# Two pairs of experts through one-hot products, and the scattered rows read back ahead of the last expert's weights

## The chip, the cores and the metric

One core of one Trainium2 chip. The metric is the device time of one execution, in microseconds (us). Three runs of the kernel before gave 2037.6, 2043.89 and 2045.23 us, median 2043.89.

## What is computed

Two layers of a hybrid network work on 512 latent tokens and 256 context tokens of width 1024. Each layer has a mixer (neighbourhood attention, a gated linear recurrence, differential attention) and then a mixture of 32 experts. Layer 0 sends all 768 tokens through the experts, layer 1 (the last) only the 512 latent ones. Each token goes to two experts:

```python
    for l in range(DEPTH):
        last = l == DEPTH - 1
        ...
        if last:
            xl = xl + ga2 * hierarchical_moe(hl2.reshape(B * S, D), *moe_args).reshape(B, S, D)
        else:
            ...
            y = hierarchical_moe(jnp.concatenate([hl2.reshape(B * S, D), hc2.reshape(B * L, D)], axis=0), *moe_args)
            xl = xl + ga2 * y[:B * S].reshape(B, S, D)
            xc = xc + cga2 * y[B * S:].reshape(B, L, D)
    return rmsnorm(xl, g_final)
```

An expert is `w2 @ (silu(w1 x) * (w3 x))` with 512 hidden columns, so its weights are 6 MB, and both layers read all of them from DRAM.

## The kernel before

The residual `X` stays in SBUF as tiles of 128 tokens by 1024 columns, six in layer 0 and four in layer 1. The experts run in an order `seq`, worked out from how many rows each may get (its capacity, 128, 64 or 32). This text counts experts by their place in that order: 0 to 31. The last ones have capacity 32, and two neighbours of these, such as 28 and 29 or 30 and 31, share a `Group` of 64 rows.

**The loop over experts** (L1973 to L2080) issues in pass n the weights of expert n (`load`, L1812 to L1823, through `eparts`, L1015 to L1026) and computes expert n-1. SP issues all these transfers from one queue: six parts of 1 MB per expert (two of w1, two of w3, two of w2), each into the next tile of a rotation `wcycle` (L1008), 16 tiles in layer 0 and 18 in layer 1. A part waits until the tile 16 or 18 places back has been used. The last expert's w2 is cut by halves of the output columns instead of halves of the rows. In layer 1 the load of expert 31 also fetches the vector `g_final`, whose tile comes from the same memory (L1820 to L1823).

**An expert** is a first product on TensorE (`first`, matmuls of w1 and w3 into `pss`), a copy to SBUF on ScalarE (`mid`), a transposition through TensorE with the activation and the product of the two halves (`hidden`; DVE writes `hT`, L1678), and a second product with w2 (`second`). `out` weighs the rows by the routing weight, into `u`.

**The rows get back to their tokens in two ways.** A `Group` with a `slot` sends its rows `u` with an indirect DMA from POOL to a DRAM buffer `yd` with two places per token (`send`, L1515 to L1518). A `Group` without one splits its rows into a high and a low part (`split`: cast on ScalarE L434, subtraction on DVE L435), makes a one-hot matrix of 64 rows by all tokens (`hots`, L1584), and multiplies the two (`product`, L1590): one product of 128 tokens by 512 columns per half tile into PSUM (`acc`, `po`), which DVE adds into `X`. For an inner group that is `add` (L1593 to L1602), a generator put on `queue`, which `fill` runs a step at a time between the matmuls of the expert after; for the last pair it is `combine` (L2094 to L2099) at the very end. Before the change only the last pair (30, 31) goes this way.

**The read-back** (L1986 to L1991) brings `yd` back after all scatters: six transfers of 1 MB in layer 0, four in layer 1, each with the two places of a tile's tokens. DVE adds them to `X` at L2110 to L2112, two adds of 128 by 1024 per tile, 12 and 8 in all.

**What sets the order.** Each engine runs its own instructions in a fixed order. Around the end of layer 0 it is spelled by a string (`LTS`, L63): a letter is a step of the last two experts, and `c` is `fill(1)`. In layer 1 the general code (L2054 to L2080) spreads the steps. The end of the last expert is `end` (L1745 to L1755): per column half a ScalarE copy L1752, a DVE add L1753, the weighing and the split, and then the 12 or 8 products of `combine`. In layer 0 two chunks of the next layer's input weights (`chunk`, L390) are loaded behind the read-back; ScalarE casts them and POOL subtracts (L435), on the engine that also makes the next layer's norm factors `rsx` (L406 to L409), from which DVE makes `dg` (L571) and ScalarE `hf` (L600) for the next layer's input product (L491).

Of the kernel before, what the change touches and what calls it, by code (L numbers as in the profile page):

```python
# [23 lines left out]
NE = 32  # L24
# [85 lines left out]
LAM = (1, 1)  # L110
DIAG = (1, 1)
SCT = (1, 1)
YLB = (3, 3)
WPRE = (4, 3)
WPS = ("ss", "sa")
# [135 lines left out]
def program(tc, a, out, dbg=None):  # L251
# [24 lines left out]
    Y = nc.sync  # L276
# [11 lines left out]
    yd = [dr.tile([2 * n_, D], F32, name=f"yd{l}") for l, n_ in enumerate((NT, NL))]  # L288
# [55 lines left out]
    def wtile(pool=None, n=6, dt=F32):  # L344
        return (pool or wt).tile([128, 2048], dt, name="w", bufs=n)
# [85 lines left out]
    ct = lambda c_, x_, y_: x_ if c_ else y_  # L431
# [20 lines left out]
    for l in range(2):  # L452
        last = l == 1
# [553 lines left out]
        wcount, held = [0], [None]  # L1007
        wcycle = [(lambda: wta, NWA[l])] * NWA[l] + [(lambda: wt2, nw2)] * nw2 + [(lambda: wt3, 4)] * 4  # L1008
# [478 lines left out]
        slots = wk_.tile([128, ncol], I32, name="slots") if SCT[l] else None  # L1487
# [21 lines left out]
        def place(s):  # L1509
            return s if s < nm else nm + (s - nm) // 2 if s < nr else s - np_  # L1510

        def column(s):
            return idn[:, place(s), :]
# [458 lines left out]
        gfin, es, early, backs = [], [], [], {}  # L1972
        for n_ in range(NE + 1):  # L1973
            f = None
            if n_ < NE:
                s = seq[n_]
                load(n_)
                if small_[0] is not None:
                    g, small_[0] = small_[0], None
                else:  # L1980
                    g = Group(column(s), slots[:, place(s):place(s) + 1] if SCT[l] and n_ < NE - 2 else None)
                    small_[0] = g if capacity(l, s) == 32 else None
                f = make(n_, g)
                es.append(f)
                g.apart = APT[l] and n_ >= NE - 2
            if n_ == NE - 1 and SCT[l]:  # L1986
                for t in ct(last, (0, 1, 2, 3), (4, 5, 0, 1, 2, 3)):
                    pl, nb = wcycle[wcount[0] % len(wcycle)]
                    backs[t] = wtile(pl() if callable(pl) else pl, nb).rearrange("p (c f) -> p c f", c=2)
                    wcount[0] += 1  # L1990
                    Y.dma_start(backs[t], yd[l].rearrange("(c t p) d -> t p c d", c=2, p=128)[t])  # L1991
            if n_ == NE - 1:
                mark.clear()
                if not last:
# [22 lines left out]
            nb = {32: 2, 64: 4, 128: 8}[e.cap]  # L2017
# [145 lines left out]
```

## Time and profile before

| what | value |
|---|---|
| runs | 2043.89, 2045.23, 2037.6 us; median 2043.89 |
| profiled execution | 2047.19 us, span 2045.6 us |
| PE (TensorE matmul) | 1692.9 us busy, 83% |
| DVE (VectorE) | 901.0 us, 44% |
| ACT (ScalarE) | 575.3 us, 28% |
| POOL (GpSimd) | 407.1 us, 20% |
| expert weights | 382 transfers of 1 MB |
| read-back | 10 transfers of 1 MB |
| scatters | 47 indirect DMAs, 44.3 us on POOL |

Spans and starts are microseconds from the start of the profiled execution's span. An engine's busy share is over the whole span. A row of a timeline has a start and a duration; what stands in brackets behind it is how long the engine had been idle and what ended that.

### The profile page before, as it was taken

To read this page: it belongs to the slowest core of one execution; us is meant where nothing else is said; L and a number is where in the kernel's file an instruction comes from. 1 tells how busy PE (TensorE), PEld (TensorE's weight loads), DVE (VectorE), ACT (ScalarE), POOL (GpSimd) and SP (SyncE) were. 2 spreads that over 40 slices of the span, in tenths; PEclk is the share of its full clock that TensorE was granted. 3 is DMA by queue.
4 is the path that set the end of the run, shared out by engine and by line. 5 is a ranking of instruction groups with operands and counts; after the bars stand their busy time and mean duration, and the time that the engine had idled before them with its cause. 6 is when DMAs were issued, how large, how long until landed. Compare 5 with 4: busy or idle time off the path is not lost. (4 is left out here: it accounts for less than half of the span.)

```text
span 2045.6 us, 24880 instructions
## 1 busy us (share of the span) xinstructions
PE 1692.9 (83%) x9306; PEld 975.2 (48%) x9306; DVE 901.0 (44%) x1506; ACT 575.3 (28%) x1033; POOL 407.1 (20%) x394
## 2 busy tenths in 40 slices
PE   4998998899697888889895987887959988879773
PEld 3766666676333333333333977566733333333221
DVE  3876443785622212212227698548662122121225
ACT  3563343662111101111113475346411010010011
POOL 1344000443311011001003145104321110010001
PEclk8999999898698998999896989898969989999886
DMA  8537967606799989989986113346469999999994
GB/s 299 203 131 285 322 225 185 165 37 252 275 409 348 407 344 368 417 325 410 401 342 261 58 51 103 125 111 207 188 228 400 404 414 409 410 413 416 416 392 167
DMA packets 153709, 579.20 MB, mean 283 GB/s; under 512 B 18734, under 2 KB 54958, under 8 KB 114672
## 3 DMA queue, kind: packets, MB, share of 16 engines
q1 hardware_dynamic: 142240, 553.35, 71.5%
q0 software_dynamic: 9328, 20.87, 2.9%
q10 hardware_dynamic: 2016, 3.34, 0.5%
q8 instruction: 75, 1.23, 0.2%
q14 instruction: 50, 0.41, 0.1%
HBM read 544.74 MB, written 42.05 MB: 287 GB/s over the span
## 5 line engine op out<-in xcount | busy, mean ns | idle before, releaser
L491 PE MATMUL mm<-hh,w 128*128 128x256 f32 (+1 forms) x960 | 191.5, 343 | 6.6 <-ACT w L434 4.7
L1643 PE MATMUL pss<-w,xT 128*64 128x512 f32 x368 | 170.7, 611 | 7.3 <-DMA w<-in_w_dram 7.3
L1642 PE MATMUL pss<-w,xT 128*64 128x512 f32 x368 | 175.3, 619 | 0.0
L1638 PE MATMUL pss<-w,xT 128*32 128x512 f32 x880 | 140.4, 686 | 37.2 <-DMA w<-in_w_dram 37.2
L491 PEld LDWEIGHTS mm<-hh,w 128*128 128x128 f32 x960 | 150.1, 193 | 37.7 <-issue 9.8
L1826 POOL DMA_INDIRECT xg<-h2d,idx_t x64 | 61.4, 959 | 515.7 <-PE mm L1628 476.8
L1648 PE MATMUL pss<-w,xT 128*128 128x512 f32 x352 | 156.0, 597 | 0.0
L1658 ACT COPY hs<-pss 128x512 f32<-128x512 f32 x53 | 30.9, 582 | 375.6 <-PE pss L1638 221.9
L1517 POOL DMA_INDIRECT yd<-yl,slots x47 | 44.3, 942 | 383.1 <-DVE yl L1562 204.3
L1700 PE MATMUL pss<-w,hT 128*64 128x512 f32 x184 | 102.0, 698 | 9.2 <-DVE hT L1678 8.9
L1648 PEld LDWEIGHTS pss<-w,xT 128*128 128x128 f32 x352 | 65.3, 190 | 89.1 <-issue 83.3
L1678 DVE TENSOR_TENSOR hT<-hT,mm 128x128 f32<-128x128 f32 (+1 forms) x53 | 18.3, 345 | 196.0 <-ACT hT L1677 195.9
L1701 PE MATMUL pss<-w,hT 128*64 128x512 f32 x184 | 102.0, 698 | 0.0
L1558 DVE SCALAR_TENSOR_TENSOR yl<-g,wsl,yl 64x1024 f32<-64x1024 f32 (+2 forms) x32 | 40.8, 1276 | 129.9 <-ACT yl L1553 129.6
L1638 PEld LDWEIGHTS pss<-w,xT 128*32 128x32 f32 x880 | 32.0, 122 | 137.7 <-issue 74.5
L1553 ACT ACTIVATE yl<-g,wsl 64x1024 f32<-64x1024 f32 (+2 forms) x32 | 36.6, 1147 | 211.2 <-DMA yd<-yl,slots 178.6
L1706 PE MATMUL pss<-w,hT 128*128 128x512 f32 x176 | 91.0, 664 | 3.1 <-issue 3.1
L491 PE MATMUL mm<-hl,w 128*128 128x256 f32 (+1 forms) x480 | 93.2, 336 | 0.1
L1562 DVE TENSOR_TENSOR yl<-pss,yl 64x512 f32<-64x512 f32 (+1 forms) x44 | 29.6, 687 | 138.7 <-PE pss L1701 76.0
L351 DVE COPY xT<-mm 128x512 f32<-128x512 f32 (+1 forms) x64 | 36.2, 566 | 101.2 <-PE mm L1628 100.5
L491 PEld LDWEIGHTS mm<-hl,w 128*128 128x128 f32 x480 | 75.4, 190 | 11.1 <-issue 0.8
L1643 PEld LDWEIGHTS pss<-w,xT 128*64 128x64 f32 x368 | 48.8, 140 | 60.3 <-issue 48.2
(377 smaller groups left out, 3263.4 us busy)
## 6 DMA issues: line engine op xcount, KB each, us to landing
w<-in_w_dram SPq DMA_DIRECT2D x382, 1024.0 KB
w<-in_w_ada_dram SPq DMA_DIRECT2D x48, 1024.0 KB
w<-in_w_in_dram SPq DMA_DIRECT2D x20, 1024.0 KB
yd<-bm SPq DMA_DIRECT2D x20, 512.0 KB
w<-yd SPq DMA_DIRECT2D x10, 1024.0 KB
ks<-st SPq DMA_DIRECT2D x16, 384.0 KB
w<-in_w_out_dram SPq DMA_DIRECT2D x5, 1024.0 KB
h2d<-hp SPq DMA_DIRECT2D x10, 512.0 KB
```

The lines of the kernel that those rows point to most:

```text
L491: i_ = T.matmul(o, x_(k), y_(k), start=(n == 0), stop=(n == 23))
L1517: G.indirect_dma_start(out=yd[l][0:2 * nrow, :], out_offset=bass.IndirectOffsetOnAxis(ap=idxt, axis=0), in_=rows, in_offset=None, bounds_c ...
L1553: S.activation(self.u[r], g2[r, 1], AF.Copy, scale=b_)
L1558: (V if eng[1] == "V" else G).scalar_tensor_tensor(self.u[r], g2[r, 0], a_, self.u[r], op0=ALU.mult, op1=ALU.add)
L1638: T.matmul(ph[32 * g:32 * g + 32, 0:512], xT[:, k + g // 2, 0:32], w(k + g // 2), start=(k == 0), stop=(k == 6))
L1642: T.matmul(ph[0:64, 0:512], xT[:, k, 0:64], w1(k), start=(k == 0), stop=(k == 7))
L1643: T.matmul(ph[64:128, 0:512], xT[:, k, 0:64], w3(k), start=(k == 0), stop=(k == 7))
L1648: T.matmul(ph[:, o:o + 512], xT[:, k, :], w(k), start=(k == 0), stop=(k == 7))
L1700: T.matmul(py[0:64, :], hT[:, k, 0:64], w2(k, 0), start=(k == 0), stop=(k == 3))
L1701: T.matmul(py[64:128, :], hT[:, k, 0:64], w2(k, 1), start=(k == 0), stop=(k == 3))
L1706: T.matmul(self.p[:, 512 * hf:512 * hf + 512], hT[:, k, :], w2(k, hf), start=(k == 0), stop=(k == 3))
L1826: G.indirect_dma_start(out=o[0:n_, :], out_offset=None, in_=h2d[l][0:nrow, :], in_offset=bass.IndirectOffsetOnAxis(ap=idxt, axis=0), bound ...
```

## The change

A constant `LATE` of 4 for both layers replaces the 2 that decides which experts get no `slot`: the pair (28, 29) now also goes through one-hot products, by the inner way (`add` on `queue`). Its rows are no longer sent to `yd`. The loop that issues the read-back moves from behind `load` of the last expert to ahead of it, in the same pass, and takes its tiles of the rotation there. Lines of the changed kernel behind the new constant are one higher.

```diff
@@ -110,6 +110,7 @@
+LATE = (4, 4)
@@ -1972,23 +1973,23 @@
         for n_ in range(NE + 1):
             f = None
+            if n_ == NE - 1 and SCT[l]:
+                for t in ct(last, (0, 1, 2, 3), (4, 5, 0, 1, 2, 3)):
+                    pl, nb = wcycle[wcount[0] % len(wcycle)]
+                    backs[t] = wtile(pl() if callable(pl) else pl, nb).rearrange("p (c f) -> p c f", c=2)
+                    wcount[0] += 1
+                    Y.dma_start(backs[t], yd[l].rearrange("(c t p) d -> t p c d", c=2, p=128)[t])
             if n_ < NE:
                 s = seq[n_]
                 load(n_)
                 if small_[0] is not None:
                     g, small_[0] = small_[0], None
                 else:
-                    g = Group(column(s), slots[:, place(s):place(s) + 1] if SCT[l] and n_ < NE - 2 else None)
+                    g = Group(column(s), slots[:, place(s):place(s) + 1] if SCT[l] and n_ < NE - LATE[l] else None)
                     small_[0] = g if capacity(l, s) == 32 else None
                 f = make(n_, g)
                 es.append(f)
                 g.apart = APT[l] and n_ >= NE - 2
-            if n_ == NE - 1 and SCT[l]:
-                for t in ct(last, (0, 1, 2, 3), (4, 5, 0, 1, 2, 3)):
-                    pl, nb = wcycle[wcount[0] % len(wcycle)]
-                    backs[t] = wtile(pl() if callable(pl) else pl, nb).rearrange("p (c f) -> p c f", c=2)
-                    wcount[0] += 1
-                    Y.dma_start(backs[t], yd[l].rearrange("(c t p) d -> t p c d", c=2, p=128)[t])
             if n_ == NE - 1:
```

Three places where the order of instructions moves. First DVE at the end of layer 0's experts, before: `hT` of L1678 is the last expert's hidden activation, L1753 its two output halves, L2112 the adds of the read-back, L2099 those of the last pair's products.

```order
L1584 TENSOR_SCALAR w<-cs_83,idn 128x128 x2
L1678 TENSOR_TENSOR hT<-hT,mm 128x4x32
L1753 TENSOR_TENSOR yl<-pss,hs 32x512
L1562 TENSOR_TENSOR yl<-yl 32x512
L1753 TENSOR_TENSOR yl<-pss,hs 32x512
L435 TENSOR_TENSOR w<-yl,w 32x512
L2112 TENSOR_TENSOR X<-X,w 128x1024
L1562 TENSOR_TENSOR yl<-yl 32x512
L2112 TENSOR_TENSOR X<-X,w 128x1024 x2
L2099 TENSOR_TENSOR X<-X,pss 128x512
```

The same place of the changed kernel (L1602 is the add of an inner group's product, L2113 that of the read-back):

```order
L2113 TENSOR_TENSOR X<-X,w 128x1024
L1679 TENSOR_TENSOR hT<-hT,mm 128x4x32
L1602 TENSOR_TENSOR X<-X,acc 128x512
L1602 TENSOR_TENSOR X<-X,po 128x512
L2113 TENSOR_TENSOR X<-X,w 128x1024 x9
L1754 TENSOR_TENSOR yl<-pss,hs 32x512
L1563 TENSOR_TENSOR yl<-yl 32x512
L1754 TENSOR_TENSOR yl<-pss,hs 32x512
L1563 TENSOR_TENSOR yl<-yl 32x512
L436 TENSOR_TENSOR w<-yl,w 32x512 x2
L2100 TENSOR_TENSOR X<-X,pss 128x512 x2
```

Nine adds of the read-back now stand between the last expert's `hT` and its output halves; before, all twelve stood behind the second half.

PE at the same place. Before, the last expert's first product (`pss<-w,xT` x16) is followed at once by its hidden step (`mm<-cst,hs`):

```order
L267 MATMUL pss<-w,hT 32x512 x8
L267 MATMUL pss<-w,xT 32x512 x16
L267 MATMUL mm<-cst,hs 128x64 x8
L267 MATMUL pss<-w,hT 32x512 x8
L267 MATMUL pss<-w 128x512 x2
```

In the changed kernel:

```order
L268 MATMUL acc<-yl,oneh 128x512
L268 MATMUL po<-yl,oneh 128x512
L268 MATMUL pss<-w,xT 32x512 x16
L268 MATMUL acc<-yl,oneh 128x512
L268 MATMUL po<-yl,oneh 128x512
...
L268 MATMUL mm<-cst,hs 128x64 x8
L268 MATMUL acc<-yl,oneh 128x512
L268 MATMUL po<-yl,oneh 128x512
L268 MATMUL pss<-w,hT 32x512 x8
```

Of the pair's twelve products two stand ahead of the last expert's first product, eight (three pairs are left out) between it and the hidden step, two behind that.

SP at the end of layer 1's experts. Before:

```order
L1024 DMA w<-in_w_dram 128x2x1024
L1822 DMA w<-in_g_final_dram 128x1024
L1818 TENSOR_LOAD sid
L1024 ISA
L1024 DMA w<-in_w_dram 128x2048
...
L1024 DMA w<-in_w_dram 128x4x512
L1991 DMA w<-yd_65 128x2x1024 x4
```

In the changed kernel:

```order
L1025 DMA w<-in_w_dram 128x2x1024
L1981 DMA w<-yd_65 128x2x1024 x4
L1823 DMA w<-in_g_final_dram 128x1024
L1819 TENSOR_LOAD sid
L1025 ISA
L1025 DMA w<-in_w_dram 128x2048
```

The four read-backs stand ahead of `g_final` and of the last expert's six parts. In layer 0 the six read-backs move likewise.

## Rows read from the trace of the kernel before

**Rows 1.** The page: DMA in 40 slices of the span.

```profile
DMA  8537967606799989989986113346469999999994
```

**Rows 2.** Windows at layer 0's end: PE, PEld, DVE, ACT, POOL, clock, DMA share, GB/s.

```profile
1060.00:1076.00 16.00, 13.96 (x127) 6.54 (x126) 8.00 (x17) 3.95 (x8) 0.91 (x1) 1.00 1.02 408
1076.00:1096.00 20.00, 10.50 (x34) 3.18 (x33) 10.73 (x16) 2.67 (x5) 0.00 (x0) 0.62 1.03 405
1096.00:1106.00 10.00, 2.42 (x4) 0.98 (x4) 10.00 (x11) 1.87 (x3) 1.30 (x14) 0.50 0.08 27
```

**Rows 3.** Windows at the end of layer 1's experts.

```profile
1985.00:2008.00 23.00, 15.09 (x96) 6.04 (x91) 4.65 (x8) 3.54 (x7) 0.00 (x0) 0.85 1.01 407
1997.00:2002.00 5.00, 4.48 (x24) 1.18 (x27) 0.00 (x0) 0.00 (x0) 0.00 (x0) 0.50 1.03 405
2008.00:2015.00 7.00, 3.34 (x17) 0.86 (x11) 3.46 (x5) 1.77 (x3) 0.00 (x0) 1.00 0.31 128
```

**Rows 4.** DMA issues from 1900 to the end: transfers, KB each.

```profile
w<-in_w_dram SPq DMA_DIRECT2D x33, 1024.0 KB
```

**Rows 5.** Waits of SP's queue, 1044 to 1110: total, times, longest.

```profile
SPq L1991 <- DMA yd<-yl,slots: 14.1, 1, 14.1
```

**Rows 6.** Timeline of POOL, 1044 to 1070: start, duration, line.

```profile
1047.65 0.92 POOL L1517 DMA_INDIRECT yd<-yl,slots  x1 [5.02 <-DVE yl L1562]
1067.54 0.91 POOL L1517 DMA_INDIRECT yd<-yl,slots  x1 [18.98 <-DVE yl L1562]
```

**Rows 7.** Timeline of PE, layer 0: expert 31's first product, hidden, second product.

```profile
1070.65 3.62 PE L267 MATMUL pss<-w,xT 128*32 128x512 f32 x32
1075.50 2.04 PE L267 MATMUL mm<-cst,hs 128*128 128x64 f32 x16 [1.23 <-ACT hs L1658]
1078.22 3.63 PE L267 MATMUL pss<-w,hT 128*32 128x512 f32 x8 [0.69 <-DVE hT L1678]
```

**Rows 8.** Timeline of DVE, layer 0: last expert's output and the adds into X.

```profile
1082.56 0.68 DVE L1753 TENSOR_TENSOR yl<-pss,hs 32x512 f32<-32x512 f32 x1 [4.39 <-ACT hs L1752]
1090.99 2.36 DVE L2112 TENSOR_TENSOR X<-X,w 128x1024 f32<-128x1024 f32 x2
1102.83 0.68 DVE L2099 TENSOR_TENSOR X<-X,mm 128x512 f32<-128x512 f32 x1
1114.76 0.69 DVE L2099 TENSOR_TENSOR X<-X,po 128x512 f32<-128x512 f32 x1 [1.70 <-PE po L267]
```

**Rows 9.** Groups by line on DVE, 1060 to 1118: the one-hot matrix.

```profile
L1584 DVE TENSOR_SCALAR w<-cs,idn 128x128 fp32r<-128x128 f32 x6 | 1.3, 274 | 0.0
```

**Rows 10.** By source line: the read-back adds, and products (min/median/max ns).

```profile
L2112 DVE TENSOR_TENSOR X<-X,w x20: 1215/1219/1226, 1089.0 to 2025.9; 128x1024 f32<-128x1024 f32 x20
L1590 PE MATMUL acc<-yl,oneh x2: 393/593/793, 2014.8 to 2026.1; 128*128 128x512 f32 x2
```

**Rows 11.** Groups by line on POOL, 1080 to 1118: busy, mean ns, idle before.

```profile
L435 POOL TENSOR_TENSOR w<-w 128x2048 fp32r<-128x2048 f32 x2 | 9.1, 4540 | 0.9 <-ACT w L434 0.9
```

**Rows 12.** Timeline of ACT and PE: first hf, then layer 1's steady input product.

```profile
1114.40 0.56 ACT L600 ACTIVATE hf<-mm,scol,acol 128x256 f32<-128x256 f32 x1
1127.40 0.36 PE L491 MATMUL mm<-hh,w 128*128 128x256 f32 x1
```

**Rows 13.** Window of layer 1's input product, just behind.

```profile
1128.00:1143.00 15.00, 15.00 (x128) 15.00 (x128) 6.97 (x30) 6.68 (x14) 1.83 (x3) 1.00 0.01 1
```

**Rows 14.** Timeline of PE, layer 1: experts 30 and 31.

```profile
1980.68 5.43 PE L1638 MATMUL pss<-w,xT 128*32 128x512 f32 x30 [2.13 <-DMA w<-in_w_dram]
1997.52 6.00 PE L1638 MATMUL pss<-w,xT 128*32 128x512 f32 x30 [3.91 <-DMA w<-in_w_dram]
```

**Rows 15.** Timeline of DVE, layer 1: second output half, first finished tile.

```profile
2012.90 0.69 DVE L1753 TENSOR_TENSOR yl<-pss,hs 32x512 f32<-32x512 f32 x1 [1.85 <-ACT hs L1752]
2027.07 0.68 DVE L2099 TENSOR_TENSOR X<-X,mm 128x512 f32<-128x512 f32 x1
```

**Rows 16.** Timeline of SP's queue, layer 1: parts 2 to 6 of expert 31.

```profile
1983.24 3.55 SPq L1024 DMA_DIRECT2D w<-in_w_dram  x5
```

## The prediction

> **What bounds the kernel now.** I read the span in 40 slices first. The DMA is full through the experts of layer 1 (9s from slice 31 to 39) and through the end of layer 0's (8s and 9s up to slice 21) [rows 1], so at both places where the change acts the weights come as fast as the queue carries them. The windows say when that ends. In layer 0 the share is 1.03 until 1096 and 0.08 in the 10 us after: the transfers end near 1096.8 [rows 2]. In layer 1 it is 1.01 until 2008 and 0.31 after, so the last bytes land near 2014 [rows 3]. The timelines give the rest: in both layers the last expert's first product waits for its weights, and behind it stands a tail in which DVE never rests long: in 1096 to 1106 it is busy 10.00 of 10.00 us [rows 2]. So two things count: when the last expert's weights are there, and how much DVE work stands behind them on the path.
>
> **The change part by part.** The sum is made against the profiled execution, 2047.19 us with a span of 2045.6, which stands 3.3 us above the median of the runs. T1 is the end of the last expert's first product: 1070.65 + 3.62 = 1074.27 in layer 0 [rows 7], 1997.52 + 6.00 = 2003.52 in layer 1 [rows 14].
>
> *(a) Layer 0, weights later.* Six read-backs, 6.29 MB, now go ahead of expert 31's six parts. At 405 to 408 GB/s [rows 2] that is 15.4 us; the pair's 64 rows of 4 KB are not written to DRAM any more, 0.26 MB or 0.6 us. T1: +14.8, to 1089.1. The wait of 14.1 us in which SP held the read-back for the pair's scatter [rows 5] gives nothing back: the queue was full meanwhile [rows 2], because 31's parts stood ahead of it. Now the read-back waits for expert 27's scatter instead, issued at 1047.65. The pair's was issued at 1067.54 [rows 6] and let the read-back go some 6 us later by the end of that wait, so I take 1054 for 27's; the queue's backlog then is several parts of 2.6 us each (1.05 MB at 405 GB/s), so it should not run dry.
>
> *(b) Layer 0, T1 to the first output half.* Before, L1753 ends at 1082.56 + 0.68 = 1083.24 [rows 8], 9.0 us after T1. Now PE has eight one-hot products before the hidden step. They alternate between two PSUM tiles, so DVE's adds pace them, which start 0.6 us apart where they run back to back (0.68 busy [rows 8], ends overlapping): 5.4 us with the first product. Then hidden 2.04 [rows 7], ACT and DVE 0.6 together, one more pair of products and adds 1.8, then the nine read-back adds that stand ahead of L1754 on DVE, 2.36 for two [rows 8] or 1.18 each: 10.6, and L1754 itself 0.68. Sum 21.1, so +12.1.
>
> *(c) Layer 0, first output half to the first complete residual tile.* Before, 1083.24 to 1102.83 + 0.68 = 1103.51 [rows 8], 20.3 us, with nine of the twelve read-back adds mixed in, 10.6 us. Without them, and with about 1 us of it lost again, 10.7 remain: the second half, the splits, the first products' adds and waits for ScalarE. So -9.6, and the tile is complete at 1120.8, +17.3.
>
> *(d) Start of layer 1.* Before, the last add ends at 1115.45 [rows 8], the first `hf` runs at 1114.40, and the steady input product only from 1127.40 [rows 12]. Between lie two chunk splits on POOL, 9.1 us [rows 11], ahead of which the norm factors could not pass. The chunks land near 1097 as before (the queue carries the same bytes), but now DVE and ScalarE get to the last tiles later than that, so the splits are over when the norm factors are wanted. I take -9.4 of it as recovered. Ends: nothing recovered (0), and all of POOL's 9.1 with the last add's own shift of only 11.4 (its read-back adds are gone), which nets +2.3 for layer 0. The value taken lies near the second end, because both splits lie on the path before. What is left is not absorbed later: PE is busy 15.00 of 15.00 us right behind [rows 13]. **Layer 0: 14.8 + 12.1 - 9.6 - 9.4 = +7.9**, bounds +2.3 and +17.3.
>
> *(e) Layer 1, weights later.* 33 parts and the read-backs share one queue here [rows 4]. Four read-backs go ahead: 4.19 MB at 407 GB/s [rows 3] is 10.3, less 0.6 for the scatter: +9.7, T1 = 2013.2.
>
> *(f) Layer 1, T1 to the first finished tile.* Before, the second half's L1753 ends at 2013.59, 10.1 after T1, and the first tile is done at 2027.75, 24.2 after T1 [rows 15]. Between the two DVE also does eight read-back adds, 1.18 each, 9.4 us. In the changed order all eight stand ahead of the last expert's `hT`, while PE still waits for weights. 10.1 + 5.3 = 15.4: -8.8. The final norm and the stores are as before. **Layer 1: +0.9**; bounds -2.5 (the first adds of the tail also come earlier) and +2 (half of a part's 2.6 us lost, see the queue below).
>
> *Covered, at nothing.* The six one-hot matrices, 1.3 us on DVE [rows 9], the pair's splits, the first two products, and three of layer 0's twelve read-back adds run while PE waits for 31's weights; without that cover they would cost 1.3, some 3, 1.2 and 3.6 us. In layer 1 the pair's eight products, 0.6 us each [rows 10], stand on PE behind the first matmul of expert 30's first product, paced by adds: about 5 us. That product waits for weights before (2.13 us, start 1980.68) and should end some 5 us later, near 1991 instead of 1986 [rows 14]. Its cover is the queue: 31's product starts at 1997.52 and would come 10 us later.
>
> **Queues passed.** The read-backs pass 31's parts on SP, and in layer 1 `g_final`'s load. That load takes a tile that expert 30's first product must have released. Before, part 2 of expert 31 was held until 1983.24 for such a tile [rows 16]; now `g_final` is held until near 1989, and all six parts stand behind it. Engines still have the backlog of 30's parts and four read-backs, several us beyond that: I take no loss.
>
> **The clock.** In layer 0, 31's product takes 3.62 us in a window of granted clock 1.00, the full 2.4 GHz [rows 2, 7]; in layer 1 a like one takes 6.00 at 0.50, 1.2 GHz, behind a PE that had waited for weights [rows 3, 14]. After the change PE waits in layer 0 too. I add nothing, since only the product's last quarter stands behind the last part, 0.6 us at most. The Trainium skill, page "TensorE: Matmul & The Clock Gate", Part 1, calls the lower clock the default, which sustained activity releases. By it the extra one-hot products on PE would argue for the full clock, and the sum would be about 1 us less; the rows here agree as far as they show the low level after waiting.
>
> **Sum.** +7.9 + 0.9 = +8.8: the profiled execution would be 2056.0, and the median 2043.9 + 8.8 = **2052.7 us**.
>
> **Rivals.**
>
> *No net change.* The start of layer 1 recovers everything it can (+2.3) and layer 1's end gains 2.5: about 2043.9. For it: 9.1 us of POOL on the path [rows 11], and transfers end when they ended before. Against it: (a) and (b) are added in a fixed order, and DVE is the engine of the tail. If the moved adds do nothing at all, it is the same number.
>
> *Slower by much: `g_final` blocks SP.* In layer 1 its load waits for expert 30's first product, which stands behind eight paced products; if that ends beyond about 1998, when the queue's backlog is eaten, every us after it delays all of expert 31 fully. Some 9 us of it, and the forecast, give 2062 or more. For it: SP was held at this tile before [rows 16]. Against: backlog of about four read-backs. The same price holds in layer 0, if 27's scatter lands past 1060.
>
> *Faster: the adds leave both tails for nothing.* If the last expert's weights were not late on the path, 20 adds of 1.18 us, 23.6, would go from the tails [rows 10]: 2043.9 - 23.6 = 2020.3. For it: DVE is full in layer 0's tail [rows 2]. Against: the queue is full, so six MB ahead must cost 15 us, and the order puts nine adds back. The Trainium skill, page "DMA: Bandwidth & Descriptors", Rules for kernel authors, says to issue a transfer early, compute, and wait late. By that rule the early read-back is right and this rival holds; the rows speak against it, with a share of 1.03 that leaves no free transfer time [rows 2].
>
> **How the numbers follow.** Forecast (net +0 to +16): 0.62. No net change: 0.20. Blocked queue: 0.12. Faster: 0.06. The range 2040 to 2062 leaves out the faster rival, the blocked queue and a little of the forecast's own upper end. Its low end is the no-change case less 3.9, its high end the forecast with nothing recovered (+9.4). A measurement tells about 0.5%, 10.2 us, from no change: faster is below 2033.7, slower above 2054.1. The forecast's 0.62 splits into 0.36 within and 0.26 above, since 2052.7 lies just inside. Same: 0.36 + 0.20 = 0.56. Slower: 0.26 + 0.12 = 0.38. Faster: 0.06.
>
> **What would show it.** In the changed kernel's profile: 31's first product ending near 1089 and 2013; nine back-to-back read-back adds in layer 0 right ahead of L1754, near 1099 to 1110; L1602 adds paced at 0.6 us ahead of the hidden step; chunk splits on POOL before the last adds, and the steady input product near 1135; `g_final`'s issue near 1989 and the DMA share still about 1.0 up to 2008. The prediction is wrong if T1 of layer 0 comes before 1084, if the nine adds run before 31's first product ends, if the input product starts by 1128, or if the DMA runs dry between 1985 and 2010.

## Result and profile after

The changed kernel took 2065.4 us (median of four runs, 2060.07 to 2074.64) against 2044.45 before; the ratio is 1.0101, 95% interval 1.0066 to 1.0136. It is slower by about 1%: 21 us between the medians, 13.5 to 27.8 us by the interval, where 8.8 were forecast. The profiled execution took 2064.35 us (span 2062.7) against 2047.19: 17.2 us more.

Executions of one kernel differ by several us before they even reach the place of the change (103 runs of the kernel before, made with the experiments below, lie between 2032.82 and 2064.15), so the traces are compared from marks close by. In layer 0 these are the start of the last gather of an expert's rows on POOL (1041.70 before, 1040.56 after), T1, the end of the first output half, the end of the first row of adds from `mm` ("tile"), and the start of the first eight steady matmuls `mm<-hl,w` of layer 1 ("steady"). In layer 1 they are its last gather (1945.43 and 1960.99), T1, tile and the end of the span. All in us:

| kernel | gather to T1 | to output half | to tile | to steady | **layer 0** | gather to T1 | to tile | to end | **layer 1** |
|---|---|---|---|---|---|---|---|---|---|
| before | 32.6 | 9.0 | 20.3 | 24.1 | 85.9 | 58.1 | 24.2 | 17.9 | 100.2 |
| forecast shift | +14.8 | +12.1 | -9.6 | -9.4 | +7.9 | +9.7 | -8.8 | 0 | +0.9 |
| changed | 47.9 | 29.6 | 12.6 | 13.6 | 103.6 | 68.7 | 16.1 | 16.9 | 101.7 |
| measured shift | +15.3 | +20.6 | -7.7 | -10.5 | +17.7 | +10.6 | -8.1 | -1.0 | +1.5 |

Layer 1 came out within 1 us of what was worked out, and in layer 0 three of four steps did within 2 us. The second step is 8.5 us larger than forecast, and layer 0 as a whole 9.8 us, so it is nearly the whole error there. The windows of the changed kernel there answer [rows 2]:

```profile
1076.00:1096.00 20.00, 13.41 (x61) 5.98 (x57) 15.22 (x25) 2.30 (x4) 0.00 (x0) 0.84 0.98 382
1096.00:1106.00 10.00, 4.63 (x13) 1.38 (x12) 9.06 (x6) 4.44 (x4) 7.15 (x2) 0.67 0.00 2
1106.00:1116.00 10.00, 0.00 (x0) 0.00 (x0) 10.00 (x6) 0.00 (x0) 3.79 (x13) 0.50 0.31 105
```

From 1106 to 1116 DVE is busy all the time and every other compute engine waits for it, with POOL busy beside it until 1109.4. DVE's timeline, columns as in [rows 8] (L2113 are the read-back adds, L1679 writes the last expert's `hT`, L1754 its first output half):

```profile
1093.94 1.22 DVE L2113 TENSOR_TENSOR X<-X,w 128x1024 f32<-128x1024 f32 x1
1096.93 0.29 DVE L1679 TENSOR_TENSOR hT<-hT,mm 128x128 f32<-128x128 f32 x1 [1.78 <-ACT hT L1678]
1098.36 18.91 DVE L2113 TENSOR_TENSOR X<-X,w 128x1024 f32<-128x1024 f32 x9
1117.30 0.68 DVE L1754 TENSOR_TENSOR yl<-pss,hs 32x512 f32<-32x512 f32 x1
```

Nine adds took 18.91 us, not 10.6. The first of the nine runs the usual time, and narrower windows show the second and third by themselves:

```profile
1099.50 5.53 DVE L2113 TENSOR_TENSOR X<-X,w 128x1024 f32<-128x1024 f32 x1
1104.95 5.51 DVE L2113 TENSOR_TENSOR X<-X,w 128x1024 f32<-128x1024 f32 x1
1110.38 4.62 DVE L2113 TENSOR_TENSOR X<-X,w 128x1024 f32<-128x1024 f32 x4
```

POOL's timeline in the same stretch, to be held beside [rows 11], where the two splits stood at 1110 and 1115, behind the last read-back add:

```profile
1098.77 10.60 POOL L436 TENSOR_TENSOR w<-w 128x2048 fp32r<-128x2048 f32 x2 [49.66 <-ACT w L435]
```

Two splits, two adds of 5.5 us; the other adds take 1.2. The splits themselves take 5.3 us on average instead of 4.54. PE and the first steady product, as in [rows 7, 12]:

```profile
1083.28 5.14 PE L268 MATMUL pss<-w,xT 128*32 128x512 f32 x30 [3.85 <-DMA w<-in_w_dram]
1093.13 3.45 PE L268 MATMUL mm<-cst,hs 128*128 128x64 f32 x16
1118.04 3.63 PE L268 MATMUL pss<-w,hT 128*32 128x512 f32 x8 [17.41 <-DVE yl L1754]
1144.14 1.12 PE L492 MATMUL mm<-hl,w 128*128 128x256 f32 x8
```

The first product ends at 1088.42, where 1089.1 was forecast; then PE waits 17.41 us for the output half on DVE. In layer 1, SP's waits from 1990 to 2010, the windows around them, and PE there, as in [rows 3, 14, 16]:

```profile
SPq L1823 <- PE pss L1639: 9.1, 1, 9.1
```

```profile
1998.00:2004.00 6.00, 5.51 (x12) 2.24 (x16) 4.93 (x9) 0.00 (x0) 0.00 (x0) 0.50 0.95 372
2004.00:2008.00 4.00, 4.00 (x20) 0.81 (x20) 1.40 (x6) 0.00 (x0) 0.00 (x0) 0.51 0.51 204
2008.00:2012.00 4.00, 3.24 (x30) 1.99 (x22) 0.00 (x0) 0.58 (x1) 0.00 (x0) 1.00 0.90 308
```

```profile
1997.76 0.79 PE L1591 MATMUL acc<-yl,oneh 128*128 128x512 f32 x1 [3.46 <-DVE yl L436]
2003.82 5.67 PE L1639 MATMUL pss<-w,xT 128*32 128x512 f32 x30
2023.79 5.92 PE L1639 MATMUL pss<-w,xT 128*32 128x512 f32 x30 [2.96 <-DMA w<-in_w_dram]
```

SP stood for 9.1 us at `g_final`'s tile, and the DMA share did fall, to 0.51 for 4 us. Expert 30's product came later than forecast: the first of the eight one-hot products had to wait 3.46 us for the split of the pair's rows (L436).

### The profile page after: what moved, and what is told of

It reads as the page before. It is cut to its first block, busy times and chain, and to the rows that moved or that the text cites. A ratio compares the mean times of both kernels' runs of the same rounds, so it can differ in the third digit from the quotient of the medians.

```text
span 2062.7 us, 24946 instructions
## 1 busy us (share of the span) xinstructions
PE 1717.8 (83%) x9326; PEld 984.3 (48%) x9326; DVE 926.2 (45%) x1540; ACT 577.3 (28%) x1037; POOL 407.9 (20%) x392
## 5 line engine op out<-in xcount | busy, mean ns | idle before, releaser
L1639 PE MATMUL pss<-w,xT 128*32 128x512 f32 x880 | 139.2, 678 | 32.7 <-DMA w<-in_w_dram 32.6
L1701 PE MATMUL pss<-w,hT 128*64 128x512 f32 x184 | 107.2, 729 | 9.3 <-DVE hT L1679 9.1
L1702 PE MATMUL pss<-w,hT 128*64 128x512 f32 x184 | 107.2, 729 | 0.0
L1679 DVE TENSOR_TENSOR hT<-hT,mm 128x128 f32<-128x128 f32 (+1 forms) x53 | 18.2, 344 | 184.9 <-ACT hT L1678 184.7
L1563 DVE TENSOR_TENSOR yl<-pss,yl 64x512 f32<-64x512 f32 (+1 forms) x44 | 29.6, 687 | 140.7 <-PE pss L1702 77.9
L1644 PEld LDWEIGHTS pss<-w,xT 128*64 128x64 f32 x368 | 49.1, 141 | 61.6 <-issue 49.4
```

What stands on the lines that cost most here:

```text
L1639: T.matmul(ph[32 * g:32 * g + 32, 0:512], xT[:, k + g // 2, 0:32], w(k + g // 2), start=(k == 0), stop=(k == 6))
L1644: T.matmul(ph[64:128, 0:512], xT[:, k, 0:64], w3(k), start=(k == 0), stop=(k == 7))
L1701: T.matmul(py[0:64, :], hT[:, k, 0:64], w2(k, 0), start=(k == 0), stop=(k == 3))
L1702: T.matmul(py[64:128, :], hT[:, k, 0:64], w2(k, 1), start=(k == 0), stop=(k == 3))
```

## The experiments

The stages of each, in the columns of the first table. T1 carries the noise of the transfers, some 2 us (3.3 once); the stages behind it repeat within 2 us where the code is the same (the second row has the kernel before in layer 0, the eighth the changed one). The times to the steady product have a weakness that matters for the last kernels and is taken up there.

| kernel | gather to T1 | to output half | to tile | to steady | **layer 0** | gather to T1 | to tile | to end | **layer 1** |
|---|---|---|---|---|---|---|---|---|---|
| e1_pair_only | 39.0 | 14.4 | 24.2 | 18.5 | 96.1 | 58.0 | 24.2 | 17.7 | 99.9 |
| e2_layer1_only | 32.6 | 8.6 | 18.6 | 25.2 | 84.9 | 70.6 | 16.1 | 17.0 | 103.8 |
| e4_split_dve | 47.9 | 21.0 | 13.1 | 14.4 | 96.4 | 68.8 | 16.1 | 17.0 | 101.8 |
| e5_split_held | 49.4 | 19.4 | 17.8 | 16.3 | 102.8 | 68.7 | 16.1 | 16.9 | 101.7 |
| e6_products_first | 47.7 | 20.4 | 14.2 | 16.4 | 98.7 | 68.8 | 16.1 | 16.3 | 101.2 |
| e8_before_gaps | 35.9 | 9.0 | 25.8 | 17.9 | 88.5 | 58.2 | 24.3 | 17.1 | 99.5 |
| e9_gaps_dve_split | 32.6 | 9.0 | 19.9 | 17.5 | 79.0 | 58.4 | 25.9 | 17.1 | 101.4 |
| e7_gfin_behind | 48.0 | 29.6 | 12.6 | 13.6 | 103.8 | 67.7 | 16.1 | 17.0 | 100.7 |
| e10_before_dve_split | 34.3 | 8.6 | 18.6 | 19.6 | 81.0 | 58.2 | 24.2 | 17.9 | 100.3 |
| e11_half_ahead | 34.3 | 8.5 | 18.6 | 19.4 | 80.8 | 61.4 | 19.4 | 17.8 | 98.7 |
| e13_half_ahead_gap | 32.6 | 8.6 | 18.6 | 19.2 | 78.9 | 61.0 | 19.4 | 17.0 | 97.5 |

**The chunk splits held back.** An edit of the changed kernel, where layer 1 takes up the two chunks:

```diff
             for c0, cut in early:
                 chunks[c0] = cut(ct(c0 in ECG, G, V))
+                tc.add_manual_dep(mark["V", "sp", c0].ins, mark["V", "hs", 1].ins.name,
+                                  mybir.DependencyInfo(mybir.DependencyClass.Sync, mybir.DependencyReason.DATA), reason="order")
```

> The changed kernel, but the two chunk splits on POOL wait for the last expert's second output half (L1754 of the changed kernel) by a semaphore; DVE's order is the same up to there. Theory (two of the nine read-back adds take 5.5 us instead of 1.2 because a chunk split runs on POOL at the time): the nine adds take 10.6 us instead of 18.9, every one near 1.2 us, and the time falls by 6 to 8 us to about 2058 us (a little may come back where layer 1 starts, since the splits now end later). Rival (the adds are slow for another reason, such as the read-back's landing): the nine adds stay at 18 us, and the time at 2065 us or above.

Measured: ratio to before 1.0075 (1.0052 to 1.0099), some 5 us less than the changed kernel but with intervals that overlap, so no gain is shown. DVE's and POOL's timelines:

```profile
1092.35 10.30 DVE L2115 TENSOR_TENSOR X<-X,w 128x1024 f32<-128x1024 f32 x9
1109.14 4.88 DVE L1565 TENSOR_TENSOR yl<-yl 32x512 f32<-32x512 f32 x1
1114.06 0.69 DVE L2102 TENSOR_TENSOR X<-X,pss 128x512 f32<-128x512 f32 x1
1116.35 2.60 DVE L436 TENSOR_TENSOR w<-yl,w 32x512 fp32r<-32x512 f32 x1
```

```profile
1108.48 9.92 POOL L436 TENSOR_TENSOR w<-w 128x2048 fp32r<-128x2048 f32 x2 [23.91 <-DVE yl L1756]
```

The nine adds are back at 10.30 us, so the splits were what stretched them. But the stretch moved with the splits: now an operation of 0.68 us takes 4.88 and another 2.60, and layer 0 is shorter by only 0.8 us (103.6 to 102.8, and by 2.3 counted from T1). Both held operations read SBUF twice; the add of L2102 between them, whose second operand is in PSUM, takes its 0.69 us while a split runs. So holding the splits is no cure, and the 6 to 8 us expected were not there.

**The chunk splits on DVE.**

```diff
-ECG = (768, 1024)
+ECG = ()
```

> The changed kernel with the two chunk splits on DVE instead of POOL (2 x 128x2048, about 2.4 us each), so that no long POOL instruction runs in layer 0's tail. Theory (while a split runs on POOL, DVE's operations with two SBUF operands wait, wherever it stands; so holding the splits only moved the loss): nine read-back adds at 1.2 us, both later splits of the one-hot rows at 0.7 us, and from the end of the last expert's first product to the first steady input product of layer 1 about 50 us instead of 55.7 (53.4 where the splits were held); some 5 to 6 us faster than the changed kernel. Rival (the tail is set by DVE's own work, the wait on POOL is hidden anyway): 55 us or more there, no faster, as DVE gets 4.8 us more work.

Measured: 1.0025 (0.9999 to 1.0050), clear of the changed kernel's interval; the median, 2054.43 us, is 9.0 us below that of the kernel with `g_final` behind (2063.42), which has the changed kernel's layer 0. From T1 to the steady product 48.5 us against 55.7, 7.2 less, although DVE got more work. DVE's groups by line, 1085 to 1135:

```profile
L2113 DVE TENSOR_TENSOR X<-X,w 128x1024 f32<-128x1024 f32 x10 | 11.5, 1218 | 0.0
L436 DVE TENSOR_TENSOR w<-w 128x2048 fp32r<-128x2048 f32 x2 | 4.6, 2292 | 0.1
L436 DVE TENSOR_TENSOR w<-yl,w 32x512 fp32r<-32x512 f32 x3 | 2.0, 682 | 0.1
```

Nothing is stretched. The step from T1 to the output half is 21.0 us, where the prediction had worked out 21.1 for the changed kernel. This is the run that settles the error: with no long POOL instruction beside DVE, step (b) comes out as worked out.

**The pair's products ahead of the last expert.**

```diff
-LTS = ("aaatmghsscccbbbbcccccMccocHccc", "")
+LTS = ("aaatmghssccccccccccccccbbbbMoH", "")
```

> The changed kernel, but in layer 0 the string of steps puts all twelve products of the pair ahead of the last expert's first product, and none between that and the hidden step; all twelve read-back adds then stand ahead of the last expert's hT on DVE. Theory: the first product still ends near 1089, hT comes late at about 1103 because DVE has 26 us of adds from 1076 on, but the output half (L1754) ends at about 1108 instead of 1118, and no add meets a chunk split: about 2055 us. Rival (the order inside the tail does not matter, only the later weights do): 2065 us.

Measured: 1.0052 (1.0030 to 1.0075). DVE:

```profile
1095.37 4.62 DVE L2113 TENSOR_TENSOR X<-X,w 128x1024 f32<-128x1024 f32 x4
1100.03 0.29 DVE L1679 TENSOR_TENSOR hT<-hT,mm 128x128 f32<-128x128 f32 x1
1113.89 3.53 DVE L436 TENSOR_TENSOR w<-yl,w 32x512 fp32r<-32x512 f32 x1
```

All twelve read-back adds are done before `hT`, each at its own time, and the output half comes 9.2 us sooner after T1 (20.4 against 29.6). A split on POOL still finds one operation of DVE to hold (3.53 us), and the whole of layer 0 is 4.9 us shorter. The order inside the tail matters, as expected, but the later weights remain.

**The pair alone.** The changed kernel with the read-back loop where it was before:

```diff
             if n_ == NE - 1 and SCT[l]:
-                for t in ct(last, (0, 1, 2, 3), (4, 5, 0, 1, 2, 3)):
...
             if n_ < NE:
                 s = seq[n_]
                 load(n_)
...
+            if n_ == NE - 1 and SCT[l]:
+                for t in ct(last, (0, 1, 2, 3), (4, 5, 0, 1, 2, 3)):
```

> Only the second one-hot pair, the read-back stays behind the last expert's weights. Theory (three costs in the changed kernel: weights later, adds ahead of the last expert's output, and DVE adds that wait while POOL splits a chunk): in layer 0 expert 31's first product ends near 1074 as before, and the eight products between it and the hidden step cost about 6 us; no add of 128x1024 takes over 1.3 us. In layer 1 g_final still holds SP behind expert 30's product, now without read-backs as backlog, some 4 us. About 2054 us. Rival (the move of the read-back is the whole cost, the pair is free): 2044 us.

Measured: 1.0032 (1.0007 to 1.0056); layer 0 is 10.2 us longer than before, layer 1 is not. In parts: T1 comes 6.4 us later, the output half 5.4 us later after it. PE and DVE:

```profile
1071.94 3.64 PE L268 MATMUL pss<-w,hT 128*32 128x512 f32 x16 [3.80 <-DVE hT L1679]
1075.51 0.80 PE L268 MATMUL acc<-yl,oneh 128*128 128x512 f32 x1
```

```profile
1108.21 6.65 DVE L2113 TENSOR_TENSOR X<-X,w 128x1024 f32<-128x1024 f32 x2
```

Of the 5.4 us the hidden step starts 3.7 later because of the eight products, and itself takes 3.51 us instead of 2.04, at a granted clock of 0.50. The 6.4 I had not expected: PE waits 3.80 us for expert 30's `hT`, which on DVE stands behind the weighing (2.58 us) and the split (1.29 us) of the pair's rows; before, it waited 0.69. Behind that wait the granted clock is 0.50 (1072 to 1076) and expert 30's second product takes 3.64 us instead of 1.92; two one-hot products add some 1.2. In the changed kernel the same wait lies under the later weights; here nothing covers it. And against my expectation an add is stretched here as well (6.65 us for two): wherever the tail is longer, it reaches the splits. In layer 1 SP waited 9.0 us for a tile that expert 30's product held, here with one of the six parts, and T1 came no later for it.

**The move alone.** The changed kernel with

```diff
-LATE = (4, 4)
+LATE = (2, 2)
```

> The read-back ahead of the last weights without the second one-hot pair: it now waits for the scatter of experts 28 and 29. Theory (SP's queue stands still until that scatter has landed, and all six parts of expert 31 behind it): in layer 0 the DMA share falls to near 0 for about 10 us, expert 31's first product ends some 25 us later than before; in layer 1 a few us of the same; 2065 to 2080 us, so the pair is what the move needs. Rival (the queue's backlog covers the wait): first product 15 us later as in the changed kernel, no dry spell, 2050 to 2060 us.

Measured: 2072.13 us in one run; 9 us of the difference lie ahead of the last gather of layer 0 (at 1051.02 instead of 1041.70). SP's waits from 1040 to 1110, the window in which the queue ran empty, and PE:

```profile
SPq L1981 <- DMA yd<-yl,slots: 20.7, 1, 20.7
```

```profile
1070.00:1080.00 10.00, 9.19 (x88) 5.56 (x88) 4.25 (x8) 1.72 (x4) 0.91 (x1) 0.99 0.01 5
```

```profile
1101.79 1.89 PE L268 MATMUL pss<-w,xT 128*32 128x512 f32 x2 [18.34 <-DMA w<-in_w_dram]
```

The DMA share is 0.01 for 10 us and the first product ends at 1112.18, 61.2 us after the last gather instead of 32.6. So the pair is what the move needs in layer 0. In layer 1 this run does not settle it:

```profile
SPq L1981 <- DMA yd<-yl,slots: 16.5, 1, 16.5
```

SP waits 16.5 us for the scatter, and the DMA share is 0.74 and 0.67 from 1995 to 2015, but T1 comes 68.6 us after the last gather, as with the pair (68.7). That gather may itself have come late: counted from layer 1's first `mm<-xl,gh`, a mark explained below, T1 takes 847.5 us, against 842.5 to 845.0 in the six kernels that have the pair and the move there. The few us expected are neither shown nor excluded.

The rest of layer 0's tail says more: with no products of a pair and all read-back adds done while PE waits, T1 to the steady product takes 35.0 us (1112.18 to 1147.15) instead of 53.3, and layer 0 in all 96.1. Some 3.4 of these 18 us are not DVE's: the two halves of the last expert's second product take 1.91 us each at a granted clock of 1.00, where they took 3.63 at 0.50 before. The rest, some 15 us, goes with the read-back adds being out of the way and no second pair. The change as it was made pays 15 us at T1, and its tail takes 55.7 us again, with the pair's products, nine adds that no longer fit ahead of them, and the held DVE.

**Layer 1 alone.** The loop stands at both places, each with its condition:

```diff
-LATE = (4, 4)
+LATE = (2, 4)
...
-            if n_ == NE - 1 and SCT[l]:
+            if n_ == NE - 1 and SCT[l] and LATE[l] == 4:
...
                 load(n_)
...
+            if n_ == NE - 1 and SCT[l] and LATE[l] == 2:
```

> The whole change in layer 1 alone, layer 0 as before. Theory (layer 0 carries nearly all of the loss): within 2 us of before, 2044 to 2047 us, although SP waits some 9 us for g_final's tile and the DMA share falls for about 4 us. Rival (SP's wait at g_final counts in full): 2053 us or more.

Measured: 1.0013 (0.9988 to 1.0038), no difference that can be told from none, and layer 0 as before within 1.1 us. The loss is in layer 0, as the theory has it; layer 1's 103.8 is the highest seen with that code (101.2 to 101.8 otherwise).

**`g_final` behind the weights.**

```diff
-                if last and n_ == NE - 1:
-                    gfin.append(wtile(wt2, nw2)[:, 0:D])
-                    Y.dma_start(gfin[0], a["g_final"].to_broadcast([128, D]))
                 wts[s] = list(eparts(v, tail=n_ == NE - 1))
+                if last and n_ == NE - 1:
+                    gfin.append(wtile(wt2, nw2)[:, 0:D])
+                    Y.dma_start(gfin[0], a["g_final"].to_broadcast([128, D]))
```

> The changed kernel with g_final's load behind the last expert's six parts instead of ahead of them; layer 0 is the changed kernel's. Theory (SP's wait of 9.1 us at g_final's tile let the DMA share fall to about 0.5 for 4 us in layer 1, which costs some 2 us): the share stays near 1.0 through that stretch, and from the last gather of layer 1 to the end it takes 99 to 100 us instead of 101.7. Rival (the backlog covers the wait in full, so it costs nothing): 101.7 us.

Measured: 1.0068 (1.0039 to 1.0096). The DMA share stays up:

```profile
2004.00:2008.00 4.00, 3.24 (x26) 0.94 (x18) 0.00 (x0) 0.59 (x1) 0.00 (x0) 0.92 1.01 409
```

and T1 of layer 1 comes 1.1 us sooner (67.7 against 68.7). So the wait of 9.1 us cost 1 us, half of what was expected, and nearly all of it was covered.

**A version that beats both?** Four kernels start from the kernel before. First, its read-back adds put where DVE waits, by ordering constraints alone:

```diff
+        sums = [V.tensor_add(X[:, t, :], X[:, t, :], backs[t][:, c_]) for t in (order if SCT[l] else ()) for c_ in range(2)]
...
+        for hf in range(2):
+            behind(mark["V", "hs", hf], sums[GAP[l][hf] - 1])
+            if GAP[l][hf] < len(sums):
+                behind(sums[GAP[l][hf]], mark["V", "hs", hf])
```

with `GAP = ((2, 5), (2, 4))`.

> The kernel before (one one-hot pair, read-back behind the last weights), with DVE's order alone changed: in layer 0 two read-back adds stand ahead of the first output half and three more ahead of the second, in layer 1 two and two; before, all stood behind. Theory (the adds can be hidden where DVE waits 4.4 and 3.6 us for the halves in layer 0, 2.7 and 1.9 in layer 1, with the read-back tiles just there): about 6 us less from the first product's end to the first complete tile in layer 0, 3 to 4 in layer 1, and 5 to 9 us less in all (a part of layer 0's may go to the chunk splits on POOL). Rival (the read-back lands too late for the gaps, so DVE waits with the output half behind it): no faster, or slower by a few us.

Measured: 0.9984 (0.9957 to 1.0011), no difference that can be told from none. DVE in layer 1 and in layer 0:

```profile
2011.77 2.49 DVE L2111 TENSOR_TENSOR X<-X,w 128x1024 f32<-128x1024 f32 x2 [1.07 <-DMA w<-yd]
```

```profile
1101.74 4.87 DVE L436 TENSOR_TENSOR w<-yl,w 32x512 fp32r<-32x512 f32 x1
```

The rival was right in layer 1: the read-back has not landed when the gap opens, and the output half waits behind it. In layer 0, where 6 us less to the tile were expected, it came 5.5 us later: the second output half stood behind a split of rows that waited 3.01 us for ScalarE, and a split on POOL stretched an operation to 4.87 us. Nothing was gained.

The same with the splits on DVE:

```diff
-ECG = (768, 1024)
+ECG = ()
```

> As the kernel with the adds in the gaps, and the two chunk splits on DVE instead of POOL. Theory (the POOL splits hold both DVE's operations on SBUF and the norm factors behind them): 2 to 4 us less than with the gaps alone, in layer 0 only, 7 to 13 us less than before in all. Rival (DVE is the engine of that tail, so 4.8 us more on it count): 2 to 5 us more than with the gaps alone.

Measured: 0.9971 (0.9942 to 0.9999); layer 0 is 6.9 us shorter, layer 1 1.2 longer. To tell which of the two edits did it, the next is the kernel before with this one edit.

> The kernel before with one edit: the two chunk splits of layer 0's tail run on DVE instead of POOL. Theory (a split on POOL holds DVE's operations on SBUF and the norm factors queued behind it, 9 us in all, while DVE does the two in 4.6 us): from the end of the last expert's first product to layer 1's steady input product 46 to 48 us instead of 53.3, the end of layer 1 as before; 5 to 7 us faster than before. Rival (the gain of the kernel with the adds in the gaps and the splits on DVE came from the gaps): 53 us there, no faster.

From T1 to the steady product it takes 46.8 us instead of 53.3, as expected. But that mark flatters this kernel: ahead of it PE has run 44 of the small matmuls `mm<-dg,X` with which layer 1 starts, where the kernel before had run 58, and the rest follow behind it. A mark without this weakness is the first `mm<-xl,gh` of layer 1 (L753), ahead of which every kernel here has run the same 408 matmuls of that start. Before, and with the splits on DVE:

```profile
1170.13 0.40 PE L753 MATMUL mm<-xl,gh 128*128 128x512 f32 x1
```

```profile
1165.01 0.40 PE L753 MATMUL mm<-xl,gh 128*128 128x512 f32 x1
```

From T1 to this mark it takes 95.9 us before and 94.8 in the other kernel with that layer 0 (the change in layer 1 alone); with the splits on DVE it takes 92.0, and 91.6 and 90.3 in the next two kernels, which have the same layer 0. So the splits on DVE are worth some 4 us there, not 6.5. With the gaps as well it is 89.5, with the gaps alone 95.2; that the gaps add some 2 us to the splits on DVE is possible, but these are single traces. By the same mark the changed kernel takes 98.7 and with its splits on DVE 91.2, 7.5 less; for the other runs above the two marks agree within 0.5 us.

The total did not follow: 1.0003 (0.9980 to 1.0027). From that mark to the last gather of layer 1 the trace takes 777.4 us, against 775.3 before; the move alone, whose splits are on POOL, takes 779.0, so this is not shown to be a cost of the edit. A gain of the splits in the total is not shown either.

Then layer 1 with only two of four read-backs ahead of the weights, `g_final` behind them as above, and layer 0 as in the last kernel:

```diff
+LATE = (2, 4)
+BACK = (0, 2)
...
+            read_back(tiles[:BACK[l]])
                 load(n_)
...
+            read_back(tiles[BACK[l]:])
```

> Layer 0 as before with the splits on DVE; layer 1 with the change, but only two of its four read-backs ahead of the last weights, and g_final's load behind them. Theory (in layer 1 each read-back ahead costs about 2.6 us at the first product's end and saves 2.4 us of adds behind it, unless the adds of those behind fit where DVE waits): the first product ends 5 us later than before, the first tile 18 to 20 us after it instead of 24.2; layer 1's end within 2 us of before, in all 5 to 8 us faster than before. Rival (the adds left behind hide completely in DVE's waits): tile 16 us after the product, 3 us faster than the kernel with the splits on DVE alone.

And last the same with two of the late adds between the output halves:

```diff
+        if last:
+            behind(sums[4], mark["V", "hs", 0])
+            behind(mark["V", "hs", 1], sums[5])
+            behind(sums[6], mark["V", "hs", 1])
+            behind(mark["V", "keep", 1, 0], mark["V", "hs", 1])
```

> As the kernel with half the read-backs ahead in layer 1 (layer 0 as before with the chunk splits on DVE), but two of the four late adds stand between the last expert's two output halves, where DVE waits 1.9 us. Theory (each gain is a few us and they add up: 5 to 7 us in layer 0, 1.5 in layer 1 as measured there, 1 to 2 more from these two adds): the first tile of layer 1's end 18 us after the product instead of 19.4, in all 6 to 10 us faster than before. Rival (the third read-back lands later than the first output half, so DVE waits and the second half with it): tile 20 us or more after the product, no better than without.

Measured: 0.9990 (0.9965 to 1.0015) and 0.9982 (0.9959 to 1.0005). In layer 1 T1 came 3.3 and 2.9 us later, not 5, and the tile 19.4 us after it in both, inside the first theory's 18 to 20; layer 1 is 1.5 and 2.7 us shorter than before. The last two adds brought nothing to the tile. By stages the last of these kernels is 9.7 us shorter than before, by the later mark 8.3; by total time no version is clearly faster than the kernel before: the interval of the one with gaps and splits on DVE ends at 0.9999, which among several versions tried says little. All four are faster than the changed kernel.

## Why the prediction was wrong

- **Weights later, (a) and (e): right.** +14.8 forecast, +15.3 measured in layer 0; +9.7 and +10.6 in layer 1, of which 1.1 is the wait at `g_final`'s tile that I had put at nothing.
- **T1 to the first output half, (b): the step that failed.** Its order of events was as forecast, row by row: the eight adds 0.6 us apart, `hT`, one more pair, nine read-back adds, L1754. The terms ahead of the nine adds came to 9.9 us for 9.8. The term of nine adds was mis-sized: "2.36 for two or 1.18 each: 10.6". They took 18.9, 8.3 more, because the two chunk splits ran on POOL at that time and held one add each. With the splits on DVE the same step took 21.0, against 21.1 worked out.
- **What was overlooked.** In (d) I moved the splits off the path and into the stretch of these adds, and put their price there at nothing: a split counted only as something ahead of which the norm factors could not pass on POOL. The trace of before held the warning, though not in the rows I showed. A `dg` operation of 0.28 us beside the second split took 3.61 us and ended with it (two of them average 1948 ns on DVE from 1110 to 1121), while adds from PSUM beside the first split took their 0.68 or 0.69. What a split does to DVE is a cost that moves with it. The rows of POOL and of DVE, and DVE's group by line, in the trace of the kernel before:

```profile
1110.09 4.56 POOL L435 TENSOR_TENSOR w<-w 128x2048 fp32r<-128x2048 f32 x1 [0.94 <-ACT w L434]
1115.52 4.52 POOL L435 TENSOR_TENSOR w<-w 128x2048 fp32r<-128x2048 f32 x1
```

```profile
1112.37 0.68 DVE L2099 TENSOR_TENSOR X<-X,po 128x512 f32<-128x512 f32 x1
1116.51 3.61 DVE L571 TENSOR_SCALAR dg<-cst,rsx 128x128 f32<-128x128 f32 x1 [1.07 <-PE mm L583]
```

```profile
L571 DVE TENSOR_SCALAR dg<-cst,rsx 128x128 f32<-128x128 f32 x2 | 3.9, 1948 | 1.9 <-PE mm L583 1.1 <-POOL rsx L409 0.9
```

The Trainium skill, page "SBUF — State Buffer", section "Who interferes with whom", states a rule: a DVE instruction with two SBUF inputs contends with a GpSimd instruction that reads SBUF, the ports that they share are locked exclusively, and the order of issue decides who blocks. The trace agrees: adds with both operands in SBUF took 5.5 us, adds with one in PSUM did not get longer, the splits, which both began while an add was running, took 5.3 us instead of 4.54, and holding the splits back only changed who waits.

An estimate from rows of before alone would have shown the risk: each of the two splits takes 4.54 us [rows 11], and if each holds one add for at most that long, step (b) lies between 21.1 and 21.1 + 2 x 4.54 = 30.2 us. 29.6 was measured.

- **Shorter tail, (c): right in direction, -7.7 for -9.6. Start of layer 1, (d): -10.5 for -9.4.** So a gain of the size that (d) expected did come, and (b) paid for it. That all of it is the splits' is not shown: three of the twelve read-back adds, 1.22 us each, ended behind the tile before and no longer do.
- **Layer 1, (f): -8.1 for -8.8.** All eight adds were done before `hT`, under PE's wait for weights.
- **The clock: too small to matter, but not nothing.** The prediction added nothing for it. In the changed kernel the granted clock was 1.00 while PE ran the eight products with short waits for DVE (1088.4 to 1093.1) and 0.51 in the 3.5 us behind them, where the hidden step took 3.45 us instead of the 2.04 in the sum. A shorter term behind it made up for that.
- **The signs named.** The nine adds did begin where forecast (1098.4 for 1099), with the splits on POOL ahead of the last adds, and ended at 1117.3 instead of 1110; the steady product ran at 1144, not 1135. The DMA share did not stay at 1.0 ahead of expert 31's parts in layer 1: it was 0.51 for 4 us.
- **The rivals.** The time, 2065.4, lies where the rival with `g_final` was put ("2062 or more"), but that mechanism cost 1 us; the agreement is chance. The faster rival fell at once: the weights were 15.3 us late.

What stays open: the medians differ by 21.0 us, the profiled executions by 17.2, and the stages by 19.2 (17.7 + 1.5); the rest is inside the spread of the executions, and I did not look for a cause in it.

## What to carry to other kernels

Before work is moved beside other work on DVE, look at what POOL does at that time: a long POOL instruction on SBUF held at most one DVE operation per instruction here, for up to its own length (1.9 to 4.3 us of 4.5 to 5.3), wherever DVE came to an operation with both operands in SBUF, so hiding it there is no hiding. A short DVE operation with a mean several times its usual one is the row to look for. And transfers moved ahead of others on a full queue cost their bytes at once (15 us for 6 MB here), so what is gained behind them must be free of its own new work: moved without the pair it took some 15 us off layer 0's tail, but the pair that makes the move possible there costs 10 by itself.

## What the runs showed of the hardware

- An add of 128x1024 with both operands in SBUF takes 1.22 us alone and 5.5 us beside a POOL subtraction of 128x2048, which itself goes from 4.54 to 5.3 us; DVE got through one add per POOL instruction. An add of 128x512 with one operand in PSUM takes 0.69 us in both cases.
- A `TENSOR_SCALAR` of 128x128 (`dg`), 0.28 us alone, took 3.61 us beside such a subtraction. It reads one tensor and one column of factors, so it is another kind than the adds; no run here takes that apart.
- The same subtraction takes 2.29 us on DVE, half of POOL's time, so two of them on DVE (4.6 us) were cheaper than letting POOL hold DVE: 7.5 us less from T1 to the first `mm<-xl,gh` of layer 1 in the changed kernel, some 4 in the kernel before.
- A wait of 9.1 us on SP's queue in front of six transfers of 1 MB cost 1.1 us at the first product that needed them: the DMA share was still 0.95 up to the last 4 us, where it was 0.51. A wait of 20.7 us in layer 0 let the share fall to 0.01 for 10 us, and the first product came 28.6 us later, where the same transfers without that wait, in the changed kernel, made it 15.3 us later.
